# Summing the last group on partitions: blocks 0 and 3 streamed through TensorE under bf16 weights, columns added and transposed on VectorE

## The chip, the cores and the metric

One core of one Trainium2 chip. The metric is the device time of one execution in microseconds (us). The kernel before was first measured at 668.67 us, the median of 3 runs (667.63 to 670.26).

## The reference, cut to what matters

```python
def setup_inputs():
    B, H, W = 4, 4224, 4224
    return {"x": np.random.randn(B, H, W).astype(np.float32)}

def reference(x):
    ps = np.cumsum(np.cumsum(x, axis=1), axis=2)
    diag = np.diagonal(ps, axis1=1, axis2=2)
    return np.cumsum(diag, axis=1).astype(np.float32)
```

Four matrices of 71 MB each. The diagonal of `ps` at place i is the sum of the square of the rows and columns up to i, and the output is the running sum of these, so every element is read once and enters a few sums. The output has 4 x 4224 numbers.

## The kernel before: the parts that matter

Each matrix is read in strips (DMA with a cast to bf16, issued by GpSimd). TensorE, ScalarE and VectorE sum each strip (a *fold* streams slices of columns through TensorE under an identity matrix and so adds them up in PSUM, the memory for its sums), and a scan over 11 groups of 384 places gives the output. In the last matrix the last group is handled apart, so that little is left to do when the last bytes land. Its rows come as `part_a` (two blocks of 128 rows, loaded in two pieces) and `part_b` (the last 128 rows as four blocks of 32, called blocks 0 to 3; block 3 comes in two pieces). This is what follows the loads, with cuts marked (P is 128, R 32, GW 384, M0 256; E0 is 352 here and 96 in the change):

```python
wp, ws = 1280, 1280 + 1536            # group before the last: fold, ScalarE, VectorE
fold_in(fold_g, strip[:, F:], 0, wp, 160, start=True)
# ... cut ...
fold_a = psum_s.tile([P, 2, 256], FP32, name="fold_a")
c0, c1 = acuts[0]                      # first piece of part_a
cp, ca = c0 + 768, c0 + 768 + 1152
fold_in(fold_a, part_a, c0, cp, 256, start=True)
# ... cut: ScalarE and VectorE sums, then the scan that gives c12 ...
c0, c1 = acuts[1]                      # second piece of part_a
cp = c0 + 768
fold_in(fold_a, part_a, c0, cp, 256)
for h in range(2):
    act_sum(asum[:, h, 3:4], part_a[:, h, cp:c1])
row_sums(asum[:, :, 4], fold_a)
row_sums(arows, asum)

def weigh(rows, w, r0, start=False):   # one row of places on one partition
    matmul(fin[:, r0:], rows, w[:, : GW - r0], start=start)

for c in range(0, CB, P):              # block 0
    matmul(by_ps, part_b[:, 0, c : c + P], weights4_h, start=c == 0)
nc.scalar.copy(out=by, in_=by_ps)
weigh(dtot, weights, M0, start=True)
weigh(ones_col, by, M0)
weigh(arows[:, 0:1], weights, 0)       # fp32, 384 columns
weigh(arows[:, 1:2], weights, P)       # fp32, 256 columns
for k, ca in ((0, 512), (1, 448)):     # blocks 1 and 2
    act_sum(bsum[:, k, 0:1], part_b[:, k + 1, :ca])
    pair_sum(bsum[:, k, 1:2], part_b[:, k + 1, ca:])
finish(0, M0)                          # yl = fin + c12, columns 0 to 255
# ... cut: weigh(bsum ...), block 3's three sums into esum, their matmuls into fin_e ...
finish(M0, GW)
nc.sync.dma_start(out=out[b, T0 : T0 + E0].unsqueeze(0), in_=yl[:, :E0])
nc.vector.tensor_add(out=ye, in0=fin_e, in1=yl[:, E0:])
nc.sync.dma_start(out=out[b, T0 + E0 : N].unsqueeze(0), in_=ye)
```

## Time and profile before

| what | before |
|---|---|
| time, median of 3 | 668.67 us |
| span of the profiled run | 665.7 us |
| TensorE, VectorE, ScalarE busy | 31%, 50%, 21% |
| load queue, share of the 16 DMA engines | 99.9% |
| end of the loads to end of the span | 3.2 us |
| last output issued to end of the span | 1.99 us |

The table is read from the bottom. The DMA engines are full until the last bytes land, so an engine's busy share over the span says nothing; only the last lines can change. The profile lines are in the prediction.

One more instant serves as a zero for all later comparisons, because the loads themselves wander by over two microseconds from run to run (the mark lies at 657.53 us in `narrow_before` and at 660.20 in `c_before2`). The **mark** is the start of TensorE's fold of the second piece of `part_a`: every version does it, when that piece lands, just ahead of the part that the change touches. In the kernel before it lies at 657.76 us. From there to the last issued output are 5.95 us, to the end of the span 7.94 us. TensorE's widest fp32 products:

```profile
657.76 0.81 PE L208 MATMUL fold_a<-strip,ident_h 128*128 128x512 bf16 x3 [0.56 <-DMA strip<-in_x_dram]
...
660.37 1.24 PE L208 MATMUL fin<-weights,arows 128*1 128x384 f32 x4
```

### The profile page before, as it was taken

Reading aid. Unit: us, or ns where it says so; the run is one execution under the profiler, and the core shown is the slowest. Engines: PE = TensorE matmul, PEld = TensorE weight load, DVE = VectorE, ACT = ScalarE, POOL = GpSimd, SP = SyncE. Lnnn points to the kernel's source line nnn. Section 1 sums busy time; section 2 is a strip of 40 time slices with the busy share of each in tenths; the row PEclk is TensorE's granted clock in tenths of the full one; section 3 lists DMA queues with packets and bytes.
Section 4 is the critical chain, followed back from the end, with each engine's and each line's share of the span. In section 5 each row is a group of like instructions: output and inputs, shape, how many; then the busy total and the mean of one; then the engine's idle time right before and its main releaser. Section 6 shows DMA issues by size and latency. Waiting matters only on the chain.

```text
span 665.7 us, 2562 instructions
## 1 busy us (share of the span) xinstructions
PE 204.5 (31%) x981; PEld 97.8 (15%) x981; DVE 334.6 (50%) x165; ACT 140.3 (21%) x226; POOL 31.3 (5%) x59
## 2 busy tenths in 40 slices
PE   0081522403117143130221623504032263250427
PEld 0030211101003021110110311202011031120203
DVE  3161625456916153454782524436288343352767
ACT  0001120406300103040630020304063002030436
POOL 7000000000000000000000000000000000001000
PEclk9995857656558585675755957666565586766758
DMA  9999999999999999999999999999999999999998
GB/s 203 219 219 219 219 218 218 219 212 207 220 221 216 219 219 215 219 215 216 212 219 222 218 215 219 216 216 218 216 213 219 221 213 220 216 216 218 218 207 162
DMA packets 7670, 143.23 MB, mean 215 GB/s; under 512 B 702, under 2 KB 1002, under 8 KB 2154
## 3 DMA queue, kind: packets, MB, share of 16 engines
q0 software_dynamic: 7296, 142.47, 99.9%
q1 hardware_dynamic: 362, 0.61, 0.3%
q8 instruction: 7, 0.11, 0.1%
q14 instruction: 5, 0.04, 0.0%
HBM read 285.47 MB, written 0.07 MB: 429 GB/s over the span
## 4 chain that ended last, share of the span: by engine, by line
DVE 47%; another core or an unknown queue 45%; DMA 5%; PE 2%; issue 1%; DVEq 0%; POOLq 0%
DVE acc L230 29%; DVE mu L320 8%; DVE strip L321 8%; DMA strip<-in_x_dram 5%; PE d L208 1%; DVE c L436 1%; PE fold L208 1%; DVE pu L230 0%; DVE c L250 0%; DVE rows L360 0%; DVE acc L335 0%; PE carry_ps L208 0%; DVE pair L239 0%; PE fin L208 0%
## 5 line engine op out<-in xcount | busy, mean ns | idle before, releaser
L208 PE MATMUL d<-strip,sel 128*11 128x384 bf16 x603 | 138.7, 403 | 377.7 <-DMA strip<-in_x_dram 377.7
L225 ACT ACTIVATE dump<-strip 128x416 bf16<-128x416 bf16 (+8 forms) x112 | 128.4, 1146 | 522.0 <-DMA strip<-in_x_dram 519.3
L320 DVE TENSOR_TENSOR mu<-strip,um 128x4608 bf16<-128x4608 bf16 (+1 forms) x24 | 52.4, 2183 | 307.1 <-DMA strip<-in_x_dram 307.0
L230 DVE TENSOR_REDUCE acc<-strip 128x6 f32<-128x4608 bf16 (+6 forms) x23 | 196.0, 8523 | 0.8
L208 PEld LDWEIGHTS <-sel 128*11 128x11 bf16 x849 | 86.2, 102 | 522.3 <-issue 479.3
L208 PE MATMUL d<-mu,sel 128*11 128x384 bf16 x243 | 49.1, 355 | 45.8 <-DVE mu L320 45.8
L321 DVE TENSOR_TENSOR strip<-strip,mu 128x4608 bf16<-128x4608 bf16 (+1 forms) x24 | 52.4, 2183 | 1.0
L76 POOL DMA_DIRECT2D strip<-in_x_dram x24 | 16.4, 686 | 543.0 <-DVE acc L230 281.7
L225 ACT ACTIVATION_READ_ACCUMULATOR dump<-strip 128x1 f32 x112 | 20.9, 186 | 0.0
L208 PE MATMUL d<-ident,rows 128*11 128x128 f32 x24 | 5.2, 379 | 16.8 <-DVE rows L369 16.8
L208 PE MATMUL fold<-strip,ident_h 128*128 128x480 bf16 x8 | 3.4, 598 | 10.7 <-DMA strip<-in_x_dram 10.7
L208 PE MATMUL d<-halves,rows 128*11 128x64 f32 x48 | 5.5, 296 | 0.0
L94 DVE MEMSET um<- 128x4608 bf16 (+1 forms) x2 | 4.9, 2458 | 1.1 <-issue 1.1
L208 PEld LDWEIGHTS d<-ident,rows 128*11 128x11 f32 x24 | 2.6, 119 | 18.5 <-DVE rows L369 11.7
L95 POOL TENSOR_SCALAR_AFFINE_SELECT um<-um 128x4608 bf16<-128x4608 bf16 (+1 forms) x2 | 5.2, 2611 | 2.4 <-DVE um L94 2.4
L208 PEld LDWEIGHTS d<-halves,rows 128*11 128x11 f32 x48 | 5.1, 134 | 1.5 <-issue 1.5
L230 DVE TENSOR_REDUCE pu<-d 11x1 f32<-11x384 f32 x4 | 2.2, 546 | 5.2 <-PE d L208 5.2
L436 DVE TENSOR_TENSOR_SCAN c<-ones_row,carry,c 11x384 f32<-11x384 f32 x4 | 4.0, 1005 | 0.1
L436 DVE TENSOR_TENSOR_SCAN c<-ones_row,carry,d 11x384 f32<-11x384 f32 x4 | 4.0, 1000 | 0.1
L409 POOL DMA_DIRECT2D strip<-in_x_dram x5 | 2.7, 557 | 26.4 <-DMA strip<-in_x_dram 26.4
L208 PEld LDWEIGHTS <-ident_h 128*128 128x128 bf16 x14 | 1.6, 119 | 13.8 <-issue 13.5
L230 DVE TENSOR_REDUCE parts<-strip 128x3 f32<-128x3072 bf16 x1 | 3.4, 3353 | 0.0
(87 smaller groups left out, 37.2 us busy)
## 6 DMA issues: line engine op xcount, KB each, us to landing
strip<-in_x_dram POOLq DMA_DIRECT2D x19, 6336.0 KB, 76.7
strip<-in_x_dram POOLq DMA_DIRECT2D x5, 3168.0 KB, 59.9
strip<-in_x_dram POOLq DMA_DIRECT2D x1, 1080.0 KB, 49.9
strip<-in_x_dram POOLq DMA_DIRECT2D x1, 768.0 KB, 52.9
strip<-in_x_dram POOLq DMA_DIRECT2D x3, 256.0 KB, 54.1
head<-in_x_dram SPq DMA_DIRECT2D x1, 528.0 KB, 4.0
strip<-in_x_dram POOLq DMA_DIRECT2D x1, 192.0 KB, 43.2
strip<-in_x_dram POOLq DMA_DIRECT2D x1, 64.0 KB, 28.6
```

The lines of the kernel that those rows point to most:

```text
L76: nc.gpsimd.dma_start(out=o, in_=x[b, r0 : r0 + f * P, :].rearrange("(p f) w -> p f w", f=f))
L94: nc.vector.memset(um, 1.0)
L95: nc.gpsimd.affine_select(out=um, in_=um, compare_op=ALU.is_gt, fill=0.0, base=0, pattern=[[-1, f], [1, f * P]], channel_multiplier=-f,)
L208: nc.tensor.matmul(o, lhsT=lhsT, rhs=rhs, start=start, stop=False, skip_group_check=True)
L225: nc.scalar.activation(out=dump[:, :w], in_=src, func=ACT.Copy, accum_out=acc)
L230: nc.vector.reduce_sum(out=acc, in_=src, axis=AX.X)
L320: nc.vector.tensor_mul(out=mu, in0=block, in1=um)
L321: nc.vector.tensor_sub(out=block, in0=block, in1=mu)
L409: nc.gpsimd.dma_start(out=part_b[:, sb, c0:c1], in_=x[b, r0 : r0 + R, :TB].rearrange("r (k c) -> r k c", k=4)[:, :, c0:c1],)
L436: nc.vector.tensor_tensor_scan(out=c12[:, i, :], data0=ones_row, data1=src, initial=carry[:, i : i + 1], op0=ALU.mult, op1=ALU.add,)
```

## The change

The intent is to leave less work behind the last landing and to hold the last 384 places on partitions, as chunks 0, 1 and 2 of 128 places each, instead of in one row. Blocks 0 and 3 are streamed through TensorE with the place weights as the loaded operand (bf16; they are whole numbers of at most 128); VectorE adds the 128 columns of the result and transposes 32x32 blocks, so that places stand in rows of 32 and can be written. The single-row adds, the ScalarE copy and block 3's sums go. TensorE folds less and ScalarE sums more.

```diff
-    wp, ws = 1280, 1280 + 1536
+    wp, ws = 1120, 1120 + 1664
-    bcut = 768
+    bcut = 640
-    cp, ca = c0 + 768, c0 + 768 + 1152
+    cp, ca = c0 + 512, c0 + 512 + 1408
-    cp = c0 + 768
+    cp = c0 + 512
 ... (arows, by, weigh, finish, esum and ye removed; asum gets a third part for dtot;
 ... chunk_rows, which issues a write of rows, and other_sums defined)
+    fin = psum_s.tile([P, 3, P], FP32, name="fold")
+    def block_cols(k, c0, c1, ps=slice(0, P), start=False):
+        w = weights4_h[:, (3 - k) * R + ps.start : (3 - k) * R + ps.stop]
+        for c in range(c0, c1, P):
+            matmul(fin[ps, 2, :], w, part_b[:, k, c : c + P], start=start and c == c0)
+    def block_sum(k):
+        w = weights4[:, (3 - k) * R : (3 - k) * R + P]
+        matmul(fin[:, 2, 0:2], w, bsum[:, k - 1, :])
+    block_cols(0, 0, CB, start=True)
+    for c in range(3):
+        matmul(fin[:, c, 0:1], c12[0:1, 1, c * P : c * P + P], ones_col[0:1, :])
+    other_sums(1, 448)                 # ScalarE and VectorE sums of block 1
+    for c in range(3):
+        matmul(fin[:, c:3, 0:5], weights[:, c * P : c * P + P], asum[:, : 3 - c, :])
+    block_sum(1)
+    other_sums(2, 384)
+    row_sums(ycols[:, 0:2], fin[:, 0:2, 0:5])          # chunks 0 and 1
+    nc.vector.transpose(out=yrows[0], in_=ycols)
+    for c in range(2):
+        chunk_rows(c, 4)                               # a write of 4 rows each
+    block_sum(2)
+    row_sums(ycols[:E0, 2:3], fin[:E0, 2, :])          # chunk 2, partitions 0 to 95
+    nc.vector.transpose(out=yrows[1][:E0, :], in_=ycols[:E0, :])
+    chunk_rows(2, 3)
+    ps = slice(E0, P)                                  # partitions 96 to 127
+    block_cols(3, 0, bcut, ps)
+    block_cols(3, bcut, CB, ps)
+    row_sums(ycols[ps, 2:3], fin[ps, 2, :])
+    nc.vector.transpose(out=yrows[2][ps, :], in_=ycols[ps, :])
+    nc.sync.dma_start(out=out[b, N - R : N].unsqueeze(0), in_=yrows[2][E0 + 2 : E0 + 3, :])
```

The weight tables grow from 128 to 224 columns so that each block finds its own shift in them.

More of the change, by code (lines that the diff above doesn't have):

```diff
@@ L195 @@
     R = P // 4
-    steps = consts.tile([P, P], I32, name="steps")
-    nc.gpsimd.iota(steps, pattern=[[4, P]], base=7, channel_multiplier=-1)
+    steps = consts.tile([P, P + 3 * R], I32, name="steps")
+    nc.gpsimd.iota(
+        steps, pattern=[[4, P + 3 * R]], base=7 - 12 * R, channel_multiplier=-1
+    )
     nc.vector.tensor_single_scalar(
@@ L200 @@
     )
-    weights4 = consts.tile([P, P], FP32, name="weights4")
+    weights4 = consts.tile([P, P + 3 * R], FP32, name="weights4")
     nc.vector.tensor_scalar_max(out=weights4, in0=steps, scalar1=0.0)
@@ L210, in matmul @@
         )
-    weights4_h = consts.tile([P, P], BF16, name="weights4_h")
+    weights4_h = consts.tile([P, P + 3 * R], BF16, name="weights4_h")
     nc.vector.tensor_copy(out=weights4_h, in_=weights4)
@@ L236, in pair_sum @@
         w = src.shape[-1] // 2
-        pair = last.tile([P, 288], FP32, name=f"pair{len(pairs)}")
+        pair = last.tile([P, 320], FP32, name=f"pair{len(pairs)}")
         pairs.append(pair)
@@ L271 @@
         nc.vector.memset(rows3[i], 0.0)
-    asum = last.tile([P, 2, 5], FP32, name="asum")
-    dtot = last.tile([P, 1], FP32, name="dtot")
+    asum = last.tile([P, 3, 5], FP32, name="asum")
+    nc.vector.memset(asum[:, 2, :], 0.0)
+    ycols = last.tile([P, 32], FP32, name="ycols")
+    yrows = [last.tile([P, 32], FP32, name=f"yrows{i}") for i in range(3)]
+    nc.vector.memset(ycols, 0.0)
     hs = last.tile([P, 3], FP32, name="hs")
@@ L282 @@
         masked(hmu[:, h, :w], head[:, h, HC - w : HC], um1[:, :w], hu[:, h : h + 1])
-    nc.vector.tensor_sub(out=asum[:, :, 0], in0=hs[:, 0:2], in1=hu[:, 0:2])
+    nc.vector.tensor_sub(out=asum[:, 0:2, 0], in0=hs[:, 0:2], in1=hu[:, 0:2])
     for b in range(B):
@@ L351 @@
                 masked(hmu[:, 2, :P], diag_b, um1[:, :P], hu[:, 2:3])
-                nc.vector.tensor_sub(out=dtot, in0=hs[:, 2:3], in1=hu[:, 2:3])
+                nc.vector.tensor_sub(out=asum[:, 2, 0:1], in0=hs[:, 2:3], in1=hu[:, 2:3])
                 for h in range(3):
@@ L421 @@
                 act_sum(asum[:, h, 1:2], part_a[:, h, cp:ca])
-            row_sums(asum[:, :, 2], part_a[:, :, ca:c1])
+            row_sums(asum[:, 0:2, 2], part_a[:, :, ca:c1])
         pu = smalls.tile([NG, 2], FP32, name="pu")
@@ L457 @@
             act_sum(asum[:, h, 3:4], part_a[:, h, cp:c1])
-        row_sums(asum[:, :, 4], fold_a)
-        arows = last.tile([P, 2], FP32, name="arows")
-        row_sums(arows, asum)
-        M0 = 2 * P
-        E0 = GW - R
-        fin = psum_s.tile([1, GW], FP32, name="fin")
-        fin_e = psum_s.tile([1, R], FP32, name="fin_e")
-        yl = last.tile([1, GW], FP32, name="yl")
-        def weigh(rows, w, r0, start=False):
-            matmul(fin[:, r0:], rows, w[:, : GW - r0], start=start)
@@ L473, in finish @@
-        def finish(c0, c1):
-            nc.vector.tensor_add(
-                out=yl[:, c0:c1], in0=fin[:, c0:c1], in1=c12[0:1, 1, c0:c1]
-            )
-        by_ps = psum_s.tile([P, P], FP32, name="fold")
-        for c in range(0, CB, P):
-            matmul(by_ps, part_b[:, 0, c : c + P], weights4_h, start=c == 0)
-        by = last.tile([P, P], FP32, name="by")
-        nc.scalar.copy(out=by, in_=by_ps)
-        weigh(dtot, weights, M0, start=True)
-        weigh(ones_col, by, M0)
-        weigh(arows[:, 0:1], weights, 0)
@@ L488 @@
-        weigh(arows[:, 1:2], weights, P)
-        bsum = last.tile([P, 2, 2], FP32, name="bsum")
-        for k, ca in ((0, 512), (1, 448)):
-            act_sum(bsum[:, k, 0:1], part_b[:, k + 1, :ca])
-            pair_sum(bsum[:, k, 1:2], part_b[:, k + 1, ca:])
-        finish(0, M0)
-        for k in range(2):
-            for i in (1, 0):
-                weigh(bsum[:, k, i : i + 1], weights4, M0 + (k + 1) * R)
-        esum = last.tile([P, 3], FP32, name="esum")
-        act_sum(esum[:, 0:1], part_b[:, 3, :320])
@@ L503 @@
-        pair_sum(esum[:, 1:2], part_b[:, 3, 320:bcut])
-        pair_sum(esum[:, 2:3], part_b[:, 3, bcut:])
-        for k in (1, 0, 2):
-            matmul(fin_e, esum[:, k : k + 1], weights4[:, :R], start=k == 1)
-        finish(M0, GW)
+        row_sums(asum[:, 0:2, 4], fold_a)
+        fin = psum_s.tile([P, 3, P], FP32, name="fold")
+        E0 = P - R
+        def block_cols(k, c0, c1, ps=slice(0, P), start=False):
+            w = weights4_h[:, (3 - k) * R + ps.start : (3 - k) * R + ps.stop]
+            for c in range(c0, c1, P):
+                matmul(
+                    fin[ps, 2, :], w, part_b[:, k, c : c + P], start=start and c == c0
+                )
@@ new lines, in block_sum, with chunk_rows @@
+        def block_sum(k):
+            w = weights4[:, (3 - k) * R : (3 - k) * R + P]
+            matmul(fin[:, 2, 0:2], w, bsum[:, k - 1, :])
+        def chunk_rows(c, k):
+            o = out[b, T0 + c * P : T0 + c * P + k * R]
+            nc.sync.dma_start(
+                out=o.rearrange("(k i) -> k i", i=R), in_=yrows[c // 2][c : k * R : R, :]
+            )
+        block_cols(0, 0, CB, start=True)
+        for c in range(3):
+            matmul(
+                fin[:, c, 0:1], c12[0:1, 1, c * P : c * P + P], ones_col[0:1, :]
+            )
@@ new lines, with other_sums @@
+        bsum = last.tile([P, 2, 2], FP32, name="bsum")
+        def other_sums(k, ca):
+            act_sum(bsum[:, k - 1, 0:1], part_b[:, k, :ca])
+            pair_sum(bsum[:, k - 1, 1:2], part_b[:, k, ca:])
+        other_sums(1, 448)
+        for c in range(3):
+            matmul(
+                fin[:, c:3, 0:5], weights[:, c * P : c * P + P], asum[:, : 3 - c, :]
+            )
+        block_sum(1)
+        other_sums(2, 384)
+        row_sums(ycols[:, 0:2], fin[:, 0:2, 0:5])
+        nc.vector.transpose(out=yrows[0], in_=ycols)
@@ L508 @@
+        for c in range(2):
[9 more added lines that the diff above has]
+        nc.vector.transpose(out=yrows[2][ps, :], in_=ycols[ps, :])
         nc.sync.dma_start(
-            out=out[b, T0 : T0 + E0].unsqueeze(0), in_=yl[:, :E0]
+            out=out[b, N - R : N].unsqueeze(0), in_=yrows[2][E0 + 2 : E0 + 3, :]
@@ L510 @@
         )
-        ye = last.tile([1, R], FP32, name="ye")
-        nc.vector.tensor_add(out=ye, in0=fin_e, in1=yl[:, E0:])
-        nc.sync.dma_start(out=out[b, T0 + E0 : N].unsqueeze(0), in_=ye)
 _INS = ['x']
```

## The prediction

> **What bounds the kernel now.** I read the busy table and the slices first, then the chain that ended last, then the stretches and the timeline of the last 7 us, because the diff only touches code after the last group of the last matrix, plus some constants at the start.
>
> From the page: the DMA row of the 40 slices, the load queue, and the chain by engine.
>
> ```profile
> DMA  9999999999999999999999999999999999999998
> ...
> q0 software_dynamic: 7296, 142.47, 99.9%
> ...
> DVE 47%; another core or an unknown queue 45%; DMA 5%; PE 2%; issue 1%; DVEq 0%; POOLq 0%
> ```
>
> The 16 DMA engines are 90% busy or more in every slice but the last, and the load queue alone fills 99.9% of their time with 142.47 MB. The chain's "another core or an unknown queue" is these loads: the timeline shows the same gaps ended by "DMA strip<-in_x_dram". VectorE's 47% lies between two landings and is hidden under the next load. So 662 us are reading x, and the change reads the same bytes. Only what follows the last landing is exposed. The stretches (us; PE, PEld, DVE, ACT, POOL busy; clock; DMA share; GB/s) say when that is:
>
> ```profile
> 661.50:662.00 0.50, 0.11 (x1) 0.00 (x0) 0.48 (x3) 0.42 (x1) 0.00 (x0) 1.00 0.81 142
> 662.00:662.25 0.25, 0.00 (x0) 0.00 (x0) 0.25 (x1) 0.25 (x2) 0.00 (x0) 1.00 0.52 70
> 662.25:662.50 0.25, 0.14 (x2) 0.14 (x3) 0.10 (x2) 0.00 (x0) 0.00 (x0) 1.00 0.15 21
> 662.50:662.75 0.25, 0.25 (x6) 0.25 (x4) 0.25 (x1) 0.23 (x1) 0.00 (x0) 1.00 0.00 0
> ```
>
> Loads are over at about 662.5; the span is 665.7, so 3.2 us are exposed. The timeline of that end (start, us, engine, line, operation, idle before and its releaser):
>
> ```profile
> 659.00 0.62 PE L208 MATMUL fold<-weights_h,strip 128*128 128x128 bf16 x8 [0.42 <-DMA strip<-in_x_dram]
> ...
> 660.15 0.16 DVE L230 TENSOR_REDUCE arows<-asum 128x2 f32<-128x10 f32 x1
> ...
> 661.52 0.46 DVE L239 SCALAR_TENSOR_TENSOR pair<-strip 128x288 f32<-128x288 bf16 x1 [0.85 <-DMA strip<-in_x_dram]
> 661.58 0.58 ACT L225 ACTIVATE dump<-strip 128x448 bf16<-128x448 bf16 x1 [0.56 <-DMA strip<-in_x_dram]
> ...
> 661.90 0.41 DVE L474 TENSOR_TENSOR yl<-fin,c 1x256 f32<-1x256 f32 x1
> ...
> 662.36 0.53 PEld L208 LDWEIGHTS fin<-weights,bsum 128*1 128x1 f32 x8 [1.26 <-DVE yl L474]
> ...
> 662.46 0.39 DVE L239 SCALAR_TENSOR_TENSOR pair<-strip 128x224 f32<-128x224 bf16 x1 [0.15 <-DMA strip<-in_x_dram]
> ...
> 662.92 0.50 PE L208 MATMUL fin_e<-weights,esum 128*1 128x32 f32 x6
> 663.12 0.28 DVE L474 TENSOR_TENSOR yl<-fin,c 1x128 f32<-1x128 f32 x1
> 663.42 0.23 SPq L508 DMA_DIRECT2D out_dram<-yl  x1
> 663.50 0.18 DVE L512 TENSOR_TENSOR ye<-fin_e,yl 1x32 f32<-1x32 f32 x1
> 663.71 0.24 SPq L513 DMA_DIRECT2D out_dram<-ye  x1
> ```
>
> Block 3, the last 32 rows, is first used at 662.46. The last output is issued at 663.71, 1.25 us later; the other 665.7 - 663.71 = 1.99 us are issue and landing of that write. So the change can work on 1.25 us, 0.19% of the time.[...]
>
> [...] 1.99 us for 128 bytes. The new last write also has 128 bytes and pays the same.[...] In the trace the bsum matmuls, which write columns 288 and up of fin, waited 1.26 us for VectorE's read of fin's columns 0 to 255, while the fin_e matmuls (another tile) ran beside the second yl.[...] The trace has no such transpose, so its cost is my estimate.
>
> **The change, part by part.** All in the clock of the trace before.
>
> Removed near the end: the 0.27 us ScalarE copy of by and its ones_col matmul (0.38), four wide arows matmuls (1.24), arows itself (0.16), both yl adds (0.41 and 0.28) and ye (0.18), block 3's two pair sums (0.39 + 0.08 and 0.29 + 0.08) and its ScalarE sum (0.47 + 0.19). VectorE work from 661.52 on was about 2.2 us.
>
> Added: block 3 becomes eight TensorE matmuls (0.62 us by the fold row); three reductions of fin and three transposes on VectorE. Reductions: the 128x10 one is 0.16 us, a 128x512 one of the trace 0.65, which gives 0.15 + 0.001 per column, so 0.28 for 128 columns. Transposes: I estimate 0.16, like a small copy (carry, 0.15). A VectorE step that reads the step before pays a gap; asum ended at 660.04, arows started at 660.15, so about 0.1.
>
> Moved: fewer folds and longer ScalarE sums. A sum grows by 0.83 ns per column (1.16 us at 1152, 1.48 at 1536), so 256 columns more cost 0.21; the two of part_a then end at about 660.15 instead of 659.7, still before block 1 lands at 660.25. The piece of block 3 cut at 640 instead of 768 changes no byte. Larger constants and three memsets fall before the first landing at 34.8 us, where VectorE sat 15.25 us idle: zero.
>
> The new end: block 2 lands at 661.5; ScalarE's 384 columns end at 662.2 and VectorE's pair of 320 columns at 662.0. The reduction of chunks 0 and 1 runs 662.03 to 662.19, the transpose to 662.44. block_sum(2) on TensorE, released by both, 662.25 to 662.5. Reduction of chunk 2, 662.55 to 662.83, transpose to 663.08. Meanwhile TensorE streams block 3's eight matmuls, about 662.4 to 663.02. Last reduction 663.1 to 663.4, gap, transpose to 663.63, issue at 663.67. Against 663.71 that is 0.04 us earlier: nothing. The saved adds and pair sums come back as reduction, gap, transpose.
>
> **The rivals.** (a) The bank wait. If the program makes block 3's matmuls wait for VectorE's read of chunk 2 although it lies on partitions 0 to 95, they run 662.88 to 663.5, the last reduction ends at 663.83, the issue comes at 664.1: 0.4 us slower. For it: the 1.26 us wait on fin in the trace, for other columns. Against: block 3 was put on partitions 96 to 127[...]. I give it a half.
> (b) The end shrinks. If the transposes are short and there are no gaps between them and the reductions, 0.3 to 0.4 us are gained. For it: VectorE has about 0.4 us less to do, and single-row adds of 256 and 384 columns vanish. Against: the last output still needs three dependent steps after the last landing, as before.
> (c) Loads disturbed: the new cut gives 2560 and 1536 byte pieces instead of 3072 and 1024, and 8 small output rows may be written while block 3 lands. 142 MB at 215 GB/s hide a few packets; I give it 0.1 us at most. A change of the DMA rate by 0.3% moves 2 us, more than everything above, and would be chance.
>
> **Range and chances.** Half of -0.04 and half of +0.4 gives +0.2 us on the kernel before. The before runs are 667.63, 668.67 and 670.26, and 667.42 in the profiled run; their mean is 668.5, so I predict 668.6. The spread of single runs is 1.3 us each way, so a median of a few runs moves by about 1 us, and the mechanism adds 0.4: 667.2 to 670.1. Two per cent is 13.4 us, ten times the spread and more than the whole 3.2 us after the last landing: same 0.98, and 0.01 on each side.
>
> **What would show it right or wrong.** Right: loads end about 3.2 us before the span does; the last output is issued 1.1 to 1.7 us after them; the last write lands 2 us after its issue; the DMA row stays at 9s. The wait before block 3's matmuls decides between me and (a): "DMA" or nothing, or "DVE ycols". A transpose far from 0.16 us or a missing gap speaks for (b). The prediction is wrong if the setup stretches past 34.8 us, if the DMA rate falls, or if the median lies beyond 2 us of before.

The sum: it came to half of -0.04 and half of +0.4, so +0.2 us on the kernel before, with the last write at the 1.99 us of the trace before and the transposes at the estimate of 0.16. "Bank wait" here and below is block 3's matmuls waiting until VectorE has read another part of the same PSUM tile; its half rested on the 1.26 us wait on `fin` in the trace and, against it, on where the change puts block 3.

## The result, and the profile after

The changed kernel took 670.11 us (median of 6, 668.88 to 671.58); the kernel before 669.03 us (median of 6, 667.62 to 670.26). The ratio is 1.002, with an interval of 1.0 to 1.0041. Ratios here are the mean time of one kernel's runs over that of the other's of the same rounds, so not quite the ratio of the medians. The median lies 0.01 us above the predicted range; that much is chance, as medians wander by far more. Two later studies gave 1.0043 (1.003 to 1.0057) and 1.002 (1.0001 to 1.0039): the changed kernel is slower, by little. The three differences of the means are 1.4, 2.9 and 1.2 us.

From the changed kernel's page, the same two rows as before (the DMA slices and the load queue):

```profile
DMA  9999999999999999999999999999999999999996
...
q0 software_dynamic: 7296, 142.47, 99.5%
```

The bytes are the same and the slices are full; only the last one is emptier (6 in place of 8), because more time passes after the loads: these end 4.7 us after the mark in both traces, which is 3.2 us before the end of the span in the kernel before and 5.35 us in the changed one. The timeline of the changed kernel's end (same columns as in the prediction; its mark is at 658.76, so 1.00 us later than before):

```profile
660.02 0.61 PE L212 MATMUL fold<-strip,weights_h 128*128 128x128 bf16 x8 [0.67 <-DMA strip<-in_x_dram]
...
660.55 1.18 PE L212 MATMUL fold<-ones_col,c 1*128 1x1 f32 x6
...
661.66 1.45 PE L212 MATMUL fold<-asum,weights 128*128 128x15 f32 x6
...
663.57 0.17 DVE L234 TENSOR_REDUCE ycols<-fold 128x2 f32<-128x10 f32 x1 [0.56 <-PE fold L212]
663.77 0.21 DVE L510 STREAM_TRANSPOSE yrows<-ycols 128x32 f32<-128x32 f32 x1
...
663.88 0.56 PE L212 MATMUL fold<-bsum,weights 128*128 128x2 f32 x2 [0.35 <-DVE ycols L234]
664.01 1.93 SPq L486 DMA_DIRECT2D out_dram<-yrows  x3
...
664.48 0.29 DVE L234 TENSOR_REDUCE ycols<-fold 96x1 f32<-96x128 f32 x1 [0.50 <-PE fold L212]
664.80 0.21 DVE L515 STREAM_TRANSPOSE yrows<-ycols 96x32 f32<-96x32 f32 x1
664.82 1.01 PE L212 MATMUL fold<-strip,weights_h 128*32 128x128 bf16 x8 [0.38 <-DVE ycols L234]
...
665.87 0.30 DVE L234 TENSOR_REDUCE ycols<-fold 32x1 f32<-32x128 f32 x1 [0.86 <-PE fold L212]
666.20 0.21 DVE L523 STREAM_TRANSPOSE yrows<-ycols 32x32 f32<-32x32 f32 x1
666.44 0.24 SPq L524 DMA_DIRECT2D out_dram<-yrows  x1
```

The last output is issued 7.68 us after the mark instead of 5.95, and lands 2.36 us later (span 668.8) instead of 1.99: 10.04 against 7.94, 2.1 us more. Three things stand out. VectorE now waits for TensorE three times (0.56, 0.50 and 0.86 us), where the prediction had TensorE ahead of it. Block 3's matmuls wait 0.38 us for VectorE's reading of chunk 2, although that reading lies on other partitions. And eight equal matmuls take 0.61 us at 660.02 but 1.01 us at 664.82, though the second eight load only 32 weight columns.

The last point has its reason in the stretches. First the kernel before, then the changed one (us; PE, PEld, DVE, ACT, POOL busy; granted clock; DMA share; GB/s):

```profile
654.00:664.75 10.75, 7.16 (x59) 3.65 (x57) 7.31 (x22) 6.55 (x15) 0.00 (x0) 0.98 0.82 153
```

```profile
654.00:660.75 6.75, 4.12 (x39) 2.52 (x37) 5.80 (x11) 5.92 (x9) 0.00 (x0) 1.00 1.10 210
660.75:666.00 5.25, 4.35 (x24) 4.02 (x23) 2.22 (x10) 1.67 (x6) 0.00 (x0) 0.51 0.36 61
```

In both, TensorE's granted clock (the share of its full clock that the trace records as granted) rises from 0.5 to 1.0 at about 654 us. In the kernel before it stays there through the last matmul, until 664.75. In the changed one it is gone at 660.9, before any of the fp32 weights of `asum` and `bsum` are loaded.

### The profile page after: what moved, and what is told of

It reads as the page before. It is cut to its first block, busy times and chain, and to the rows that moved or that the text cites. A ratio compares the mean times of both kernels' runs of the same rounds, so it can differ in the third digit from the quotient of the medians. Undisturbed runs are those within 1.5% of the kernel's fastest.

```text
span 668.8 us, 2562 instructions
## 1 busy us (share of the span) xinstructions
PE 208.0 (31%) x980; PEld 101.5 (15%) x980; DVE 334.9 (50%) x165; ACT 140.7 (21%) x223; POOL 31.4 (5%) x59
## 3 DMA queue, kind: packets, MB, share of 16 engines
q0 software_dynamic: 7296, 142.47, 99.5%
## 4 chain that ended last, share of the span: by engine, by line
DVE 48%; another core or an unknown queue 43%; DMA 5%; PE 2%; issue 1%; DVEq 0%; POOLq 0%
DVE acc L234 29%; DVE mu L327 8%; DVE strip L328 8%; DMA strip<-in_x_dram 5%; DVE c L443 1%; PE d L212 1%; PE fold L212 1%; DVE parts L234 1%; DVE pu L234 0%; DVE c L254 0%; DVE acc L342 0%; DVE rows L367 0%; PE carry_ps L212 0%; DVE ycols L234 0%
## 5 line engine op out<-in xcount | busy, mean ns | idle before, releaser
L212 PE MATMUL d<-strip,sel 128*11 128x384 bf16 x603 | 140.8, 408 | 377.5 <-DMA strip<-in_x_dram 377.5
L234 DVE TENSOR_REDUCE parts<-strip 128x3 f32<-128x3168 bf16 x1 | 3.5, 3453 | 0.0
```

The costliest lines, as they stand in the source:

```text
L212: nc.tensor.matmul(o, lhsT=lhsT, rhs=rhs, start=start, stop=False, skip_group_check=True)
L234: nc.vector.reduce_sum(out=acc, in_=src, axis=AX.X)
```

## The experiments

The table holds all 17 chip runs and the two first traces. "Clock" is from the rise of the granted clock to its fall; "issue" and "end" count from the mark; "write" is the difference of the last two, rounded on its own. Issue times of single traces are exact to some 0.02 us; ends and writes to 0.05, as spans are given to 0.1. The clock's times were read from stretches. The clock's own records in the traces say 6.83 us in every run with 6.8 to 7.0, 10.24 in every run with 10.1 to 10.3, and 13.65 in `c_before2`.

| run | clock, us | issue | end | write | ratio to before (95%) |
|---|---|---|---|---|---|
| before, first trace | 10.1 | 5.95 | 7.94 | 1.99 | |
| c_before | 10.2 | 5.93 | 7.87 | 1.94 | (no timing) |
| c_before2 | over 10.5 | 5.93 | 7.90 | 1.97 | (no timing) |
| changed, first trace | 6.8 | 7.68 | 10.04 | 2.36 | 1.0020 (1.0000 to 1.0041) |
| c_after | 6.8 | 7.05 | 9.41 | 2.36 | 1.0043 (1.0030 to 1.0057) |
| c_after2 | 6.8 | 7.07 | 9.50 | 2.43 | 1.0020 (1.0001 to 1.0039) |
| own_bank | 6.8 | 7.85 | 10.30 | 2.45 | 1.0033 (1.0018 to 1.0047) |
| wide3 | 6.9 | 7.05 | 9.40 | 2.35 | 1.0026 (1.0013 to 1.0039) |
| no_c12 | 6.9 | 7.21 | 9.56 | 2.35 | 1.0023 (1.0010 to 1.0036) |
| old_splits | 6.9 | 7.05 | 9.46 | 2.41 | 1.0024 (0.9998 to 1.0050) |
| act_queue | 6.8 | 8.23 | 10.80 | 2.57 | 1.0033 (1.0013 to 1.0053) |
| only_last | 7.0 | 8.38 | 10.29 | 1.91 | (no timing) |
| fill | 10.3 | 6.64 | 9.07 | 2.43 | 1.0003 (0.9986 to 1.0021) |
| fill_again | 10.3 | 6.89 | 9.30 | 2.41 | 1.0025 (1.0008 to 1.0042) |
| fill_one | 10.3 | about 5.95 | 8.45 | about 2.5 | 1.0010 (0.9995 to 1.0024) |
| narrow_before | 10.2 | 5.95 | 7.87 | 1.92 | (no timing) |
| splits_before | 6.8 | 7.14 | 9.12 | 1.98 | (no timing) |
| splits_before2 | 6.8 | 7.14 | 9.07 | 1.93 | 1.0011 (0.9992 to 1.0030) |
| both_before | 6.9 | 6.43 | 8.43 | 2.00 | (no timing) |

Where ratios are compared below, the runs were made on the same chip and share the runs of the kernel before.

**The two kernels again, unedited.** No edit in `c_after`, `c_after2`, `c_before` and `c_before2`.

> The changed kernel again, unedited. All times in these runs are counted from the mark: the start of TensorE's fold of the second piece of part_a, which every version does when that piece lands, just before the changed tail. In the first traces the last output was issued 5.95 us after the mark in the kernel before and 7.68 us in the changed one, and the span ended 7.94 and 10.04 us after it. My theory: the tail is longer by about 2.1 us always (issue 7.6 to 7.8, end 9.9 to 10.2), and the mark itself wanders by about 1 us by chance. Rival: the tail is as before and the whole difference is a DMA stream that starts later: then the tail would differ from the first trace by more than 1 us. Ratio expected 1.003, between 1.000 and 1.006.

> The changed kernel unedited, to stand in one call beside the two below. Theory: ratio to the kernel before 1.002 to 1.005 as in its first two studies; clock lost 6 to 7 us after its rise; last issue 7.0 to 7.7 us after the mark, end 9.4 to 10.1.

> The kernel before, unedited, for a second trace. Theory: its granted TensorE clock rises just after 654 us and stays at 1.0 for about 10 us, through the last matmul, as in the first trace (654.5 to 664.75), because its wide matmuls keep TensorE busy; all five traces of kernels with the changed tail lost the clock 6.8 us after it rose. Last issue 5.9 to 6.0 us after the mark, end 7.9 to 8.0. Rival: the early fall of the clock is chance and comes in this kernel too; then the last issue would be 0.2 or more later. The first load's landing (34.8 us before, 36.6, 36.6, 36.6, 34.3 and 34.9 in the five others) is chance in my theory; I expect either value.

> The kernel before, a third trace. Theory: the second period after the rise holds 40% of streaming or more whatever its start, so the clock stays 10 us and the last issue is 5.9 to 6.0 us after the mark. Rival: with an early start of the period it falls below and the clock is lost after 6.8 us here too.

The kernel before repeats itself to 0.02 us in the issue: 5.95, 5.93, 5.93. The changed kernel does not: 7.68, 7.05, 7.07, and `c_after` missed the issue and the end that I had expected. Its tail is longer in every trace, though, by 1.5 to 2.2 us; the mean ends are 9.65 and 7.90 us after the mark, 1.75 apart. The mean of the three timed differences is 1.8 us. So the tail is enough to account for the time.

The first load landing is chance, as expected. First the kernel before in its second trace, then the changed kernel in its third (start and length of VectorE's first use of a strip):

```profile
36.77 2.56 DVE L320 TENSOR_TENSOR mu<-strip,um 128x4608 bf16<-128x4608 bf16 x1 [17.20 <-DMA strip<-in_x_dram]
```

```profile
34.71 2.56 DVE L327 TENSOR_TENSOR mu<-strip,um 128x4608 bf16<-128x4608 bf16 x1 [14.84 <-DMA strip<-in_x_dram]
```

Of the 19 traces, 11 have that landing between 34.3 and 35.3 us and 8 between 36.6 and 37.0, and both kernels are in both groups. What decides it is open.

**Block 3 in a PSUM tile of its own (`own_bank`).**

```diff
-        block_cols(3, 0, bcut, ps)
-        block_cols(3, bcut, CB, ps)
-        row_sums(ycols[ps, 2:3], fin[ps, 2, :])
 ... (tiles fin3, q3 and both, and the weights w3, defined)
+        for c in range(0, CB, P):
+            matmul(fin3[ps, :], w3, part_b[:, 3, c : c + P], start=c == 0)
+        nc.vector.tensor_copy(out=q3[ps, :], in_=fin[ps, 2, :])
+        nc.vector.scalar_tensor_tensor(out=both[ps, :], in0=fin3[ps, :], scalar=1.0,
+            in1=q3[ps, :], op0=ALU.mult, op1=ALU.add, accum_out=ycols[ps, 2:3])
```

> Block 3 goes to a PSUM tile of its own, so TensorE needs not wait until VectorE has read chunk 2; VectorE copies the earlier part of the last quarter out beforehand and adds it in the last reduction. Theory (the bank wait costs 0.4 us): block 3's matmuls start right after block_sum(2), some 0.4 us earlier than in the changed kernel, and the last issue comes 0.2 to 0.4 us earlier (7.3 to 7.5 us after the mark; the last reduction is 0.1 longer). Rival (TensorE is simply the bound, or VectorE's queue is): the last issue stays at 7.6 to 7.8.

The timeline of that run:

```profile
664.47 0.56 PE L212 MATMUL fold<-bsum,weights 128*128 128x2 f32 x2 [0.35 <-DVE ycols L234]
...
664.96 1.03 PE L212 MATMUL fin<-strip,weights_h 128*32 128x128 bf16 x8
665.07 0.29 DVE L234 TENSOR_REDUCE ycols<-fold 96x1 f32<-96x128 f32 x1 [0.50 <-PE fold L212]
...
665.63 0.30 DVE L526 COPY q<-fold 32x128 f32<-32x128 f32 x1
```

The wait is gone: block 3's matmuls run beside VectorE's reading of chunk 2. They end 0.96 us after block_sum(2) does, where the changed kernel's first trace has 1.39. But the issue comes at 7.85, not at 7.3 to 7.5. The clock had fallen even earlier here (1.5 us after the mark, 2.1 in the first trace), VectorE's extra copy and accumulator reading took time, and SyncE was still issuing the other writes until 666.53. So the run shows that the wait is real and costs about 0.4 us on TensorE; it does not show a gain. Nor does it tell what part of PSUM the wait goes by, since the edit gives block 3 a tile of its own.

**Block 3 under all 128 weight columns (`wide3`).**

```diff
-        block_cols(3, 0, bcut, ps)
-        block_cols(3, bcut, CB, ps)
+        block_cols(3, 0, bcut)
+        block_cols(3, bcut, CB)
```

> Block 3's matmuls with all 128 weight columns instead of 32 (the other columns are zeros). Theory (a load of 32 columns[...] took 0.10 us each, the load of 128 columns 0.054): the eight matmuls fall from 1.01 to about 0.62 us and the last issue comes about 0.4 us earlier, 7.3 us after the mark. Rival (the matmuls are spaced by waiting for VectorE or by the clock): they stay at 1.0 us.

```profile
663.04 1.01 PE L212 MATMUL fold<-strip,weights_h 128*128 128x128 bf16 x8 [0.38 <-DVE ycols L234]
```

The theory that the narrow weights cost the time fell at once: with 128 columns the eight matmuls take 1.01 us as well. The rival named the clock. In five traces of changed tails it fell 6.8 to 6.9 us after it rose, and never so in the kernel before.

**Without the c12 matmuls (`no_c12`, wrong).** The edit deletes the loop with `c12` in the diff above.

> The three one-row matmuls that add c12 to the last group are left out, so the last 384 values of the last matrix are wrong on purpose. Theory (TensorE's queue of fp32 weight loads is what delays the reading of chunks 0 and 1): asum's three matmuls start when asum is complete, about 0.45 us earlier, and everything after moves with them: last issue at 7.2 to 7.3 us. Rival (block 2's sums or the bank waits set it): last issue unchanged within 0.1.

The asum matmuls start 2.44 us after the mark, 0.46 earlier than the 2.90 of the first trace, and the issue is at 7.21, as expected. But 7.05 was reached by the unedited `c_after` too, where the clock fell later (3.8 us after the mark, here 1.4). TensorE's queue counts; how much of it in the usual case this run can't say, as the two effects mix.

**Fillers that keep TensorE streaming (`fill`, `fill_again`).** Ten matmuls of 512 columns into a spare tile, at four places where TensorE would idle:

```diff
+            def fill(n):
+                for _ in range(n):
+                    matmul(junk, ident_h, part_a[:, 0, 1536:2048], start=True)
+            fill(2)                                    # after the first folds of part_a
         matmul(carry_ps[:, 1:2], apart, pu[:, 0:1])
+        if not whole:
+            fill(3)
+        fill(2)
         block_cols(0, 0, CB, start=True)
         block_sum(1)
+        fill(3)
```

> The changed kernel with ten useless matmuls of 512 columns into a spare PSUM tile where TensorE idles in the last 10 us (two before carry, three after it, two before block 0, three before block_sum(2)). Theory (the clock falls because the changed tail streams too few columns): the clock stays at 1.0 until after block 3, the six asum instructions take 0.83 us instead of 1.45, block_sum 0.38 instead of 0.56, block 3's eight matmuls 0.62 instead of 1.01, and the last issue comes about 6.4 to 6.7 us after the mark in place of 7.05 to 7.68. Rival (the fall of the clock is a timer, whatever the work): the clock falls 6.8 us after its rise as in the five traces, and the last issue is at 7.0 or later.

> The changed kernel with ten filler matmuls, again. In its first trace the clock stayed 10 us, the last issue came 6.64 us after the mark and the end 9.07. Theory: the same within 0.2, and a ratio to the kernel before 0.001 to 0.0015 below that of the changed kernel in this call (0.4 to 1.0 us); the difference may be too small to clear the noise of the loads. Rival (first result was luck): clock lost after 6.8 us, ratio as the changed kernel.

The stretch of `fill` up to the fall of the clock, then lines of its timeline:

```profile
653.75:663.75 10.00, 8.43 (x68) 5.41 (x67) 7.19 (x20) 6.83 (x14) 0.00 (x0) 1.00 0.89 165
```

```profile
660.32 0.83 PE L212 MATMUL fold<-asum,weights 128*128 128x15 f32 x6
...
662.96 0.61 PE L212 MATMUL fold<-strip,weights_h 128*32 128x128 bf16 x8 [0.38 <-DVE ycols L234]
...
664.37 0.33 SPq L535 DMA_DIRECT2D out_dram<-yrows  x1
```

More work on the engine makes it faster: the clock stays for 10.3 us, the asum matmuls fall from 1.45 to 0.83 us and block 3's from 1.01 to 0.61, and the issue comes at 6.64. So the fall is no timer but depends on what TensorE does. In `fill_again` the clock fell just before block 3 (664.32 against 664.67), so that those took 1.01 us again, and the issue was at 6.89. In timed runs the gain does not show clearly: 1.0003 beside 1.0024 and 1.0033 of two unfilled versions, but 1.0025 beside 1.0020 of the changed kernel. The wandering of the loads covers it.

**Which part of the change loses the clock (`old_splits`, `narrow_before`, `splits_before`, `splits_before2`, `both_before`).** `old_splits` takes the old division back in the changed kernel; `splits_before` puts the new one into the kernel before and changes nothing else:

```diff
-            wp, ws = 1280, 1280 + 1536
+            wp, ws = 1120, 1120 + 1664
-            cp, ca = c0 + 768, c0 + 768 + 1152
+            cp, ca = c0 + 512, c0 + 512 + 1408
-        cp = c0 + 768
+        cp = c0 + 512
```

`narrow_before` takes the stream time of the wide fp32 products out of the kernel before (wrong, though the comparison did not object, presumably because these terms are small beside the carried sums). `both_before` is both.

```diff
-        arows = last.tile([P, 2], FP32, name="arows")
+        arows = last.tile([P, 2], BF16, name="arows")
-        weigh(arows[:, 0:1], weights, 0)
-        weigh(arows[:, 1:2], weights, P)
+        weigh(arows[:, 0:1], um1, 0)
+        weigh(arows[:, 1:2], um1, P)
```

> The changed kernel with the old division of part_a and the group before it between TensorE's folds and ScalarE (three folds of 512 columns instead of two, twice, and eight of 480 instead of seven). Theory: if the folds taken away are enough to explain the clock, it now stays for 10 us and the last issue is at 6.5 to 6.8 us after the mark. Rival: the wide fp32 matmuls of arows were what kept it, the folds alone do not help, and the last issue is at 7.0 to 7.7 as in the changed kernel. I lean to the rival.

> The kernel before with its two wide arows products in bf16 and with a mask of ones in place of the fp32 weights (wrong on purpose): the same 384 and 256 columns and waits, but a quarter or so of the streaming time (1.24 us before). Theory (these wide fp32 products are what keeps the granted clock for a third period): the clock now falls 6.7 to 7.0 us after it rose, as in the nine traces of the changed tail without fillers, where the kernel before and the filled ones had 10.1 to 10.3; last issue 6.0 to 6.3 us after the mark. Rival (another part of the change, the folds or the tail's fp32 weight loads, loses the clock): it stays 10 us.

> The kernel before with the change's division of part_a and of the group before it (two folds of 512 columns instead of three, twice; seven of 480 instead of eight), nothing else. Theory: the clock stays 10 us, last issue 5.9 to 6.1 us after the mark. Rival: the folds taken away lose it.

> Both edits together. Theory: the clock falls 6.7 to 7.0 us after its rise, last issue 6.0 to 6.4 us after the mark. If only this run loses the clock, neither edit is enough alone and it takes the sum of the streaming that was removed.

> The kernel before with the change's division of folds alone, again and timed. Its first look lost the clock after 6.75 us and issued the last output 7.14 us after the mark instead of 5.95, against my expectation. New theory: the clock of a 3.4 us period is lost when TensorE streams columns for about a third or less of the period before it (counted from the traces: at most 34% in the eleven that lost it after the second period, at least 40% in the six that kept it). With two folds instead of three the second period holds 25 to 35%: the clock falls 6.7 to 7.0 us after its rise, last issue 6.3 to 7.2 us after the mark, ratio to the kernel before 1.0005 to 1.002. Rival (the first look was chance and depends on where the period starts): it stays 10 us, last issue 5.9 to 6.1.

In `old_splits` the rival held: the old folds alone don't bring the clock back. My theory for the other side did not hold: without the wide products the one trace of `narrow_before` still kept the clock (10.2 us, issue unmoved), though by a hair, as the count below shows; and the new division alone loses it (`splits_before`: 6.8 us), again in `splits_before2`, as that expectation said. `both_before` lost it too. The stretches of `splits_before`, and from its timeline the products and the last issue:

```profile
653.50:660.00 6.50, 3.95 (x38) 2.15 (x35) 5.55 (x11) 5.64 (x9) 0.00 (x0) 1.00 1.09 209
660.00:663.50 3.50, 2.74 (x7) 0.59 (x6) 1.35 (x7) 2.34 (x9) 0.00 (x0) 0.51 0.67 116
```

```profile
660.84 2.34 PE L208 MATMUL fin<-weights,arows 128*1 128x384 f32 x4
...
665.02 0.24 SPq L513 DMA_DIRECT2D out_dram<-ye  x1
```

In the kernel before, moving one fold of 512 columns of each piece (and one of 480 before them) from TensorE to ScalarE halves the clock for the 3.4 us in which TensorE has most to do: the fp32 products take 2.34 us instead of 1.24, and the tail is 1.2 us longer. A smaller part has another cause: ScalarE's longer sums hold up its copy of `by` by 0.39 us, and with it the start of these products by 0.35. So one piece of the change costs that much without touching a line of the tail. Timed, this is 1.0011 with an interval that holds 1.

The common rule is a count. It was made from the traces: the columns that TensorE streamed in the second 3.41 us after the rise, as a share of what 2.4 columns per ns would give, with an fp32 column as four. Both figures are rounded from spacings in the first trace of the kernel before, at clock 1.0: the matmuls of 512 bf16 columns start 0.215 us apart (2.38 columns per ns); a product of 384 fp32 columns stands there as two matmuls, which start 0.322 us apart, so that a column costs 4.0 times as much. (With their tail, 640 fp32 columns took 1.24 us, 4.65 by the same count.) The count is an estimate. The period is read from the traces: 6.83 and 10.24 us are two and three times 3413 ns, and every change of the clock in a trace lies on one grid of 3413 ns to within 2 ns. No long idle stretch is needed for the fall: in the changed kernel's two periods at full clock TensorE never sat idle for more than 0.7 us (first trace). In the twelve traces that lost the clock after the second period, its share of streaming is 17 to 32% (`old_splits` 32, `splits_before` 31, changed 17 to 26); in the seven that kept it, 36 to 72% (before 59 to 69, `narrow_before` 36, `fill_one` 39).

The same count over whole traces (columns laid out from each matmul's recorded start) bears it out. From 40 us on, the 19 traces hold 954 periods at full clock. The 381 after which the clock fell have a share of at most 35.6%; the 573 after which it stayed have at least 35.9%. No period is on the wrong side. (In the two first traces the clock fell after 40 periods of at most 34.6% and stayed after 60 of at least 37.0%.) With an fp32 column counted as one to three there are exceptions, and TensorE's busy time in place of the columns leaves 15. So in these traces about 36% of the columns of a period (some 2,900 of 8,192) hold the clock, and `narrow_before` was just above: by this count, a period starting 0.6 to 1.0 us after its mark would have held 33 to 34%. So that trace does not acquit the wide products.

Where a period begins differs from run to run, and with it the changed kernel's tail: where the clock fell 3.8 and 3.0 us after the mark the issue came at 7.05 and 7.07, where it fell at 2.1 (first trace) at 7.68, and in `only_last`, where it fell at 1.2, at 8.38. The kernel before kept the clock in all three traces, and its issue did not move.

**The chunk writes on another queue, and not at all (`act_queue`, `only_last`).**

```diff
-            nc.sync.dma_start(                         # in chunk_rows; act_queue
+            nc.scalar.dma_start(
-        for c in range(2):                             # only_last: no chunk writes
-            chunk_rows(c, 4)
-        chunk_rows(2, 3)
```

> The three writes of chunk rows are issued by ScalarE's queue instead of SyncE's; the last write stays on SyncE's. Theory (the last write, 1.99 us from issue to end in the kernel before and 2.35 to 2.45 in the five others, waits behind chunk 2's write of 3 rows that was issued a little earlier on the same queue): it falls back to 1.9 to 2.1 us. Rival (a row read from partition 98, or a write close after any other, takes that long): it stays at 2.3 to 2.5. The issues of 0.64 us each are not on the path in either.

> The changed kernel without the three writes of chunk rows (those 352 outputs are never written, so the result is wrong on purpose); the last write stays. Theory (the other writes, close before it, stretch the last one): from the last issue to the end 1.9 to 2.1 us, as in the kernel before, instead of 2.35 to 2.45. Rival (it is the read from partition 98): 2.3 or more.

From the timeline of `only_last`, whose span is 668.1 us:

```profile
666.19 0.23 SPq L521 DMA_DIRECT2D out_dram<-yrows  x1
```

Alone, the last write takes 1.91 us from issue to end, as in the kernel before; with the three others ahead of it, 2.35 to 2.45. So it is not the read from partition 98. Whether sharing the queue does it stays open: with the others on ScalarE's queue it took 2.57, but ScalarE issued them until 666.37, after the last write's issue had begun, so that chunk 2's write may have been the one that ended last. (Issue times this late in `only_last` and `act_queue` come from an early fall of the clock.)

**Chunk 2 read once, with the fillers (`fill_one`).** On top of `fill`:

```diff
-        row_sums(ycols[:E0, 2:3], fin[:E0, 2, :])
-        nc.vector.transpose(out=yrows[1][:E0, :], in_=ycols[:E0, :])
-        chunk_rows(2, 3)
         block_cols(3, 0, bcut, ps)
         block_cols(3, bcut, CB, ps)
-        row_sums(ycols[ps, 2:3], fin[ps, 2, :])
-        nc.vector.transpose(out=yrows[2][ps, :], in_=ycols[ps, :])
-        nc.sync.dma_start(out=out[b, N - R : N].unsqueeze(0), in_=yrows[2][E0 + 2 : E0 + 3, :])
+        row_sums(ycols[:, 2:3], fin[:, 2, :])
+        nc.vector.transpose(out=yrows[1], in_=ycols)
+        chunk_rows(2, 4)
```

> The filler matmuls, and chunk 2 read once: block 3's matmuls come before any reading of chunk 2, so the wait for VectorE's reading goes away with the thing waited for; one reduction, one transpose and one write of four rows end it. Theory (the bank wait and the second reduction are on the path): block 3's matmuls start right after block_sum(2), the last transpose ends about 0.4 us earlier than in the filled kernel (mark plus 6.0 instead of 6.4), but the write of four rows costs 0.64 us to issue in place of 0.24, so the end is 8.5 to 8.9 us after the mark, still over the 7.9 of the kernel before. Rival (VectorE or SyncE's queue bounds the end): last transpose at 6.3 or later, end at 9.0 or more.

```profile
662.39 0.62 PE L212 MATMUL fold<-strip,weights_h 128*32 128x128 bf16 x8
...
663.37 0.21 DVE L531 STREAM_TRANSPOSE yrows<-ycols 128x32 f32<-128x32 f32 x1
```

Block 3's matmuls follow block_sum(2) without a wait, and the last transpose ends 5.93 us after the mark, against 6.42 in `fill`: 0.49 us for the bank wait with the second reduction and transpose behind it. The last write is issued at about 5.95, as in the kernel before: with the clock held and the wait gone, the changed tail is as fast up to there. The end is at 8.45, the best of the changed tails and still 0.55 behind the kernel before, all of it in the write. No version tried beats the kernel before.

## Why the prediction was wrong

The range was missed by 0.01 us, which is chance. The cost was not: 0.2 us was forecast, and the means differ by 1.2 to 2.9 us. The prediction's own signs say where it lies: the last output was to be issued 1.1 to 1.7 us after the loads and came 2.3 to 3.0 after them, and its write was to land in 2 us and took 2.4. By its own steps:

- **What bounds the kernel: right.** The loads fill 99.5% of the queue, and what the change does lies in the microseconds after them. "Same" at 2% held, for the reason given. But the count of what is exposed was too small: work before the last landing is exposed too, once TensorE falls behind and hands its delay on.
- **"All in the clock of the trace before": this step failed.** Every added TensorE term was costed at clock 1.0, as if the change could not alter it. It does: the clock is halved from 660.9. Block 3's term was 0.62 and measured 1.01. The prediction took a duration for a property of the instruction; here it went with the instruction and with what TensorE did in the period before.
- **The fp32 weights: mis-sized.** block_sum(2) stood at 0.25 us. It takes 0.38 at full clock and 0.56 to 0.59 at half. The three asum products and the three c12 products were not given a size at all; they take 0.83 and 0.82 us at full clock (1.45 and 1.18 in the first trace). It is the clock that makes this matter: where the clock fell later (`c_after`, `c_after2`) or was held (`fill`), chunks 0 and 1 are read 4.16 to 4.17 us after the mark without a wait, ahead of the 4.27 worked out; in the first trace at 4.81.
- **Folds and longer ScalarE sums: "moved" was taken as harmless. Wrong.** ScalarE did finish in time, as estimated. What was missed is on the giving side: `splits_before` lengthens the tail by 1.2 us, mostly through the clock.
- **Rival (a), the bank wait: it came,** 0.38 us, with VectorE's reading of chunk 2 as its releaser. Block 3's matmuls, on partitions 96 to 127, did not start before the reading of partitions 0 to 95 had ended. It had a half; it should have had more, as the wait on `fin` in the trace before was for other columns of the same tile. (That wait's 1.26 us was idle time of the weight loads; the matmuls' own was 0.76.) Its price was right: `fill_one` gains 0.49 us with it and the second reduction gone.
- **Rival (b): no gain.** The transposes take 0.21 us, not 0.16, and the gaps are 0.03 us from reduction to transpose, not 0.1; the two errors nearly cancel.
- **"The new last write pays the same": wrong by 0.4 us.** It takes 2.35 to 2.45 us after three other writes, and 1.91 alone. The forecast had taken over the 1.99 us of the trace before, where one small write stood 0.28 us ahead of the last. Nor was it foreseen that a write of 3 or 4 rows costs SyncE 0.50 to 0.72 us to issue, though this rarely lay on the path (some 0.2 us in `fill`).
- **The setup:** no effect, as said; the constants end at 19.9 us and the first load lands at 34.3 at the earliest.
- **Slips in the sums, too small to matter:** 668.5 and 0.2 make 668.7, not 668.6; and block 3's matmuls were started at 662.4 while block_sum(2), on the same engine, was to end at 662.5.

In sum, 0.2 us slower was predicted for the end. The three traces of the changed kernel say 1.75: about 0.4 in the last write, about 0.5 in the bank wait and the second reduction and transpose (`fill_one`), about 0.6 in the halved clock (the mean issue of 7.27 against 6.64 in `fill`), and 0.2 that `fill` still lost to SyncE's issuing. This is an estimate from single traces; in the timed runs the parts do not stand out from the wandering of the loads.

## What to carry to other kernels

Before taking matmuls away from a phase that is short of time, look at the granted clock of that phase and of the few microseconds before it: less streaming there halved the clock for what TensorE did next (`splits_before`: 0.51 for 3.5 us, and 2.34 us instead of 1.24 for the same products), and a duration read from one version was not valid for another. In a tail of a few microseconds, count each wait for another engine's use of the same PSUM tile (0.38 us here), each fp32 weight load (here 0.12 us for a load of 128 columns at full clock, 0.23 at half), and the extra writes near the last one (about 0.4 us here for three). And compare tails from a common landmark in the traces, because loads that wander by 2 us hide any of this in the times.

## What else the traces show

- Loads of fp32 weights with few columns to stream did not bring the clock back: in the changed kernel's first trace weight loads were busy for 4.02 of 5.25 us (660.75 to 666.00), and the clock was 0.51 in that stretch.
- Loads of 32 and of 128 bf16 columns took the same time: 0.74 us for seven at the low clock (changed kernel's first trace, `wide3`) and 0.43 at full clock (`fill`, `c_after`). Six fp32 load instructions of 128 columns took 0.74 us at full clock (`c_after`), 123 ns each, and 1.36 at half (`own_bank`), 227 ns each.
- The wait before block 3's matmuls was 0.38 us in every changed version that reads chunk 2 first and keeps block 3 in the same tile. No run here tests the hardware without that wait.
- The last write, 128 bytes issued by SyncE, took 1.91 us with no chunk write ahead of it (`only_last`), 1.92 to 2.00 in the kernel before and its variants, and 2.35 to 2.45 shortly after three others. Issuing a write of 3 or 4 rows took SyncE 0.50 to 0.72 us, and one of a single row 0.23 to 0.34.
- VectorE's transposes of 32 fp32 columns took 0.21 us on 128, 96 and 32 partitions.
